# Fixed byte offsets between the weight buffers and the moving buffers of a hybrid encoder block

## The chip, the cores and the metric

The kernel runs on one core of one Trainium2 chip. The metric is device time in microseconds (us) of one execution, the median of several; "the profiled execution" is one further execution, recorded by the hardware profiler.

## What is computed

One layer on 256 tokens of width 2048, in float32: a SwiGLU feed-forward, a token mixer (a gated depthwise convolution beside a gated DeltaNet with 8 heads), a second SwiGLU, and a final norm. Every sub-layer is conditioned by shifts, scales and gates made from a vector c.

```
mods = (silu(c) @ w_ada + b_ada).reshape(9, 2048)
h = rmsnorm(x, n1) * (1 + mods[1]) + mods[0];  x += 0.5 * mods[2] * ((silu(h @ wg1) * (h @ wu1)) @ wd1)
h = rmsnorm(x, n2) * (1 + mods[4]) + mods[3];  p = h @ w_in
x += mods[5] * (concat(conv_group(p), deltanet_group(p)) @ w_out)
h = rmsnorm(x, n3) * (1 + mods[7]) + mods[6];  x += 0.5 * mods[8] * ((silu(h @ wg2) * (h @ wu2)) @ wd2)
out = rmsnorm(x, nf)
```

The weight matrices are 2048x5632 (twice) and 5632x2048 in each feed-forward, 2048x6160 into the mixer and 2048x2048 out of it.

## The kernel before

Features lie on the 128 partitions, tokens in the free dimension (T = 256), so x is 16 tiles of 128x256. Weights stream from HBM as 1 MB tiles `raw` (`weights`, L123). `split` (L110) takes half of one, 128 x 8 x 128 floats, and makes two float32r tiles of it: `hi` on ScalarE (L113) and `lo`, the remainder, on VectorE (L115). The activations are split in the same way: an `h` tile holds the normed and modulated input of 128 features, its hi half first and its lo half behind it (`h_make` L232, `h_pre` L249, both from `h_tile` L244), and an `act` tile holds the gated product of the feed-forward (`ffn_evac` L292, `put_split` L287).

A product of two split operands is three matmuls, `mm3` (L139): L142 is (weight hi, moving hi), L143 is (weight hi, moving lo), L144 is (weight lo, moving hi). The 128x128 weights are the stationary operand, loaded by one LDWEIGHTS before each matmul; the 256 tokens are the moving operand. So from one product to the next the weights that are loaded are hi, hi, lo, hi, hi, lo, and the moving halves are hi, lo, hi.

`mm3` is called from four places that differ in how often the moving tile changes:
- `col_tile` (L344): for one output tile, 16 k tiles after each other; every three matmuls go to the next h tile. The rest of both feed-forwards' gate and up products, and the mixer's input products, are of this kind.
- the second product of a feed-forward (`ffn`, L318): the same with 22 act tiles.
- `first` (L382), the first 20 column tiles of feed-forward 1: 8 weight tiles, so 24 matmuls, for one h tile, then the next.
- `group` (L265): 6 weight tiles, so 18 matmuls, for one h tile, at the start of the mixer and of feed-forward 2; the moving rows are 258 wide there.
Together 3744 products take an h tile as the moving operand and 1408 an act tile: 15456 matmuls. (1920 of them are those of `first`.) Another 112 products of plain float32 (L888) make part of the mixer's output.

The order of the work is the tile framework's schedule of this program; TensorE runs its matmuls in that order, one queue for each engine. Loads are on SyncE's queue (`load`, L118). The weights of the conditioning (`ada`, L205) are read beside the rest at a rate set in units of weight halves (`tick`, L86).

**Where the buffers lie.** Pools are laid one behind the other in the order in which they are opened (L62 to L69), every tile of a pool at the next multiple of 32 bytes, per partition: `raw` 4 x 8192 bytes, `hi` 3 x 4096, `lo` 3 x 4096, `h` 16 x 2112, `tmp` (10 tiles of 1024 bytes, two for `rb` and one for `dg` among them, and 2 of 512), `small` 832 bytes, and then, while a feed-forward runs, `act` 22 x 2048. All sizes up to h are multiples of 256 bytes but that of an h tile, 2112 = 8 x 256 + 64. Every slice of 128 weights is 512 bytes on, and a moving lo half 1024 bytes on, so slices don't change a place modulo 256. Call **offset** the place of the weights less that of the moving rows, modulo 256. Before the change it is the same for hi and lo: 0, 192, 128 and 64 for h buffers 0, 1, 2, 3 and so on in fours, and 192 for every act buffer, as 832 is 64 more than a multiple of 256. In `group` the moving lo half lies 8 bytes further.

In the gate and up products of the two feed-forwards the h tiles take these offsets in the order 192, 0, 64, 128 from one k tile to the next. (In `first` four k in a row use the same four kinds of buffer, but tiles of any two offsets can come next to each other.) The trace gives no addresses, but its matmuls stand in the program's order, so each one's offset is known from the program: the four h tiles that `first` goes through from 135.48 us of the span have the offsets 128, 192, 0 and 64, the tile from 56.69 us has 64 after one of 192, and the k tiles from 1621.86 us have 128, 192, 0, 64 and 128. What is counted as a matmul's offset is that of the weights loaded beside it, which are the next matmul's.

Other tiles that the change touches: `dg` and `rb` of `token_rsqrt` (L180: the reciprocal root of a mean square, spread over the partitions by a matmul with ones), called five times; `cacc`, the sum of the convolution's channels (L536 to L539), and `om`, a constant matrix (L544), both in `conv_norm` (L542), which takes mean and variance of the convolution while the plain float32 matmuls of L888 run; `acc`, the running sum of squares (`squares`, L309).

Of the kernel before, what the change touches and what calls it, by code (L numbers as in the profile page):

```python
# [8 lines left out]
F32 = mybir.dt.float32  # L9
F32R = mybir.dt.float32r  # L10
I32 = mybir.dt.int32
AF = mybir.ActivationFunctionType
# [3 lines left out]
P = 128  # L16
T = 256
D = 2048
# [3 lines left out]
FH = FT // 2  # L22
# [8 lines left out]
VISITS = [(g, a[g], b[g]) for a, b in zip(((0,) * NG,) + ROUNDS, ROUNDS) for g in (range(NG)[::-1] if b is ROUNDS[-1] else range(NG)) if a[g] < b[g]]  # L31
ORDER = [g * 4 + j for g, _, end in VISITS if end == 8 for j in range(4)] + list(range(4 * NG, FH))
EPS = 1e-6

PARAMS = [
    ("b_ada", 144), ("n1", 16), ("n2", 16), ("n3", 16), ("nf", 16), ("w_dw", 8 * TAPS), ("b_dw", 8),
# [15 lines left out]
class Body:  # L52
    def __init__(self, ctx, tc, x, c, prm, e0, w_ada, wa1, gu1, wd1, wk, w_in, w_ba, w_out, gw2, gu2, wd2, out):
        nc = tc.nc
        self.nc, self.tc = nc, tc
        self.x_d, self.c_d, self.prm_d, self.e0_d, self.ada_d = x, c, prm, e0, w_ada
        self.wa1_d, self.wk_d, self.w_in_d, self.w_ba_d, self.w_out_d, self.gw2_d, self.out_d = wa1, wk, w_in, w_ba, w_out, gw2, out
        self.gu_d, self.wd_d = (gu1, gu2), (wd1, wd2)
        self.bg, self.credit, self.ready = [], 0.0, 0
        self.n = 0  # L60
        self.ordered = True
        pool = lambda name, bufs, **kw: ctx.enter_context(tc.tile_pool(name=name, bufs=bufs, **kw))  # L62
        self.pers = pool("pers", 1)
        self.rawp = pool("rawp", 4)
        self.hip = pool("hip", 3)
        self.lop = pool("lop", 3)
        self.hp = pool("hp", 16)
        self.tmp = pool("tmp", 2)
        self.small = pool("small", 2)  # L69
        self.mm = pool("mm", 4, space=bass.MemoryType.PSUM)  # L70
        self.aux = pool("aux", 2, space=bass.MemoryType.PSUM)
        self.auxd = pool("auxd", 2, space=bass.MemoryType.PSUM)
        self.dram = pool("scr", 1, space=bass.MemoryType.DRAM)

    def nm(self, s):
        self.n += 1
        return f"{s}{self.n}"
# [102 lines left out]
    def token_rsqrt(self, parts, col, beside=False, raw=False):  # L180

        nc = self.nc
        ps = self.bank(self.aux)
        for i, part in enumerate(parts):
            for s in range(2):
                nc.tensor.matmul(ps[:, s:s + 1], lhsT=part[:, s * P:(s + 1) * P], rhs=col, start=i == 0 and s == 0,
                                 stop=i == len(parts) - 1 and s == 1)
        v = self.tile(self.small, [P, 2], "nv")
        nc.vector.tensor_scalar(out=v, in0=ps[:, 0:2], scalar1=EPS, scalar2=None, op0=ALU.add)
        r = self.rsqrt(v, 2, "n", beside=beside)  # L190
        dg = self.tile(self.tmp, [P, 2, P], "dg", bufs=1)
        for s in range(2):
            if beside:
                nc.scalar.activation(out=dg[:, s, :], in_=self.ident, func=AF.Copy, scale=r[:, s:s + 1])
            else:
                nc.vector.tensor_scalar(out=dg[:, s, :], in0=self.ident, scalar1=r[:, s:s + 1], scalar2=None, op0=ALU.mult)
        pb = self.bank(self.aux)
        nc.tensor.matmul(pb[:, 0:T], lhsT=self.ones, rhs=dg, start=True, stop=True)
        if raw:
            return pb[:, 0:T]  # L200
        rb = self.tile(self.tmp, [P, T], "rb")
        self.normed = nc.scalar.activation(out=rb, in_=pb[:, 0:T], func=AF.Copy)
        return rb

# [39 lines left out]
    def h_tile(self, extra=0):  # L244

        n = T + extra
        return self.tile(self.hp, [P, 2 * T + 16], "h", F32R)[:, 0:2 * n].rearrange("p (g t) -> p g t", g=2)

    def h_pre(self, k, scale, shift):  # L249

# [273 lines left out]
    def conv_taps(self, j, xs):  # L524
        nc = self.nc
        acc = self.tile(self.cva, [P, T], "cva")
        w = lambda i: self.prm[:, PSPAN["w_dw"]][:, j * TAPS + i:j * TAPS + i + 1]
        nc.scalar.activation(out=acc, in_=xs, func=AF.Identity, scale=w(TAPS - 1), bias=self.prm[:, PSPAN["b_dw"]][:, j:j + 1])  # L528
        for i in range(1, TAPS):
            after = None if i > 1 or j < 2 else self.solved if j < 4 else self.taps[j - 2]  # L530
            with self.tc.issue_after(after.ins) if after is not None else nullcontext():
                self.taps[j] = nc.vector.scalar_tensor_tensor(out=acc[:, i:T], in0=xs[:, 0:T - i], scalar=w(TAPS - 1 - i),  # L532
                                                               in1=acc[:, i:T], op0=ALU.mult, op1=ALU.add)
            yield 0.33
        if j == 0:
            self.cacc = self.tile(self.mx, [P, T], "cacc")  # L536
            nc.gpsimd.tensor_copy(out=self.cacc, in_=acc)
        else:
            nc.gpsimd.tensor_tensor(out=self.cacc, in0=self.cacc, in1=acc, op=ALU.add)  # L539
        self.cv[j] = acc  # L540

    def conv_norm(self):  # L542
        nc = self.nc
        om = self.tile(self.mx, [P, P], "om")  # L544
        nc.gpsimd.memset(om, 2.0 / D)  # L545
        pm = self.bank(self.aux)
        nc.tensor.matmul(pm[:, 0:T], lhsT=om, rhs=self.cacc, start=True, stop=True)
        mu = self.tile(self.tmp, [P, T], "rb")
        nc.scalar.activation(out=mu, in_=pm[:, 0:T], func=AF.Copy)
        acc = self.tile(self.tmp, [P, T], "acc", bufs=1)  # L550
        for j in range(8):
            nc.vector.tensor_tensor(out=self.cv[j], in0=self.cv[j], in1=mu, op=ALU.subtract)
            self.sq_acc(acc, self.cv[j], j == 0)
            yield 0.7
        rb = self.token_rsqrt([acc], self.col2)
        yield 3.0
        for j in range(8):
            t = self.cv[j]
            nc.vector.tensor_tensor(out=t, in0=t, in1=rb, op=ALU.mult)
            nc.scalar.activation(out=t, in_=t, func=AF.Silu, scale=self.prm[:, PSPAN["ln_w"]][:, j:j + 1],  # L560
                                 bias=self.prm[:, PSPAN["ln_b"]][:, j:j + 1])
            y = self.h_tile()
            self.put_split(y, t)
            self.y[j] = y
            yield 0.8
# [15 lines left out]
    def l2(self, heads, tag, pool):  # L581
# [7 lines left out]
        v = self.tile(self.mx, [P, 16], tag + "v")  # L589
        nc.vector.tensor_scalar(out=v, in0=ps[:, 0:16], scalar1=EPS, scalar2=None, op0=ALU.add)  # L590
        return self.rsqrt(v, 16, tag, self.mx, True)
# [143 lines left out]
    def dn_out(self):  # L735
# [4 lines left out]
        for b in range(2):  # L740
# [50 lines left out]
            for s in range(2):  # L791
                u0 = (b + 2 * s) * 4
                nc.gpsimd.tensor_tensor(out=sc[:, s * 4:s * 4 + 4], in0=on[:, s * 4:s * 4 + 4], in1=self.rq2[:, u0:u0 + 4], op=ALU.mult)
            nc.gpsimd.tensor_scalar(out=sc, in0=sc, scalar1=1.0 / P, scalar2=EPS, op0=ALU.mult, op1=ALU.add)
            r = self.rsqrt(sc, 8, "o", beside=True)
# [110 lines left out]
    def all(self):  # L906
        nc, tc = self.nc, self.tc
        self.rate = 0.0
        n = self.norms = {}
        with tc.tile_pool(name="actp", bufs=FH) as self.actp, tc.tile_pool(name="spp", bufs=2) as self.spp, \  # L910
                tc.tile_pool(name="adap", bufs=2) as self.adap:
            self.start()
            self.bg = [self.ada_task(2), self.ada_task(4, n["n2"]), self.ada_task(3), self.ada_task(5), self.ada_task(6)]
            done = self.first()
            self.rate = 0.44
            self.ffn(0, 2, done, lambda m: self.h_pre(m, 4, 3))
            self.drain()
        self.ordered = False
        self.mix(lambda m: self.h_pre(m, 7, 6))
        with tc.tile_pool(name="actp2", bufs=FH) as self.actp, tc.tile_pool(name="spq", bufs=6) as self.spq:  # L920
            made = self.group(self.gw2_d, self.parts, 7, 6, lambda: self.tile(self.spq, [P, T], "hq"))
            done = [self.ffn_evac(t, u, b, v) for (t, b), (u, v) in zip(made, made)]
            self.rate = 0.25
            self.bg, self.credit = [self.ada_task(8)], -5
            self.ffn(1, 8, done, self.weigh)
            rb = self.token_rsqrt(self.parts, self.col, raw=True)
            for a, b in OUTS:
                xs = self.x[:, a:b, :]
                nc.vector.tensor_tensor(out=xs, in0=xs, in1=rb.unsqueeze(1).broadcast_to([P, b - a, T]), op=ALU.mult)
                nc.sync.dma_start(out=self.out_d[:, a:b, :], in_=xs)  # L930
# [67 lines left out]
```

## Time and profile before

| | us |
|---|---|
| median of 3 executions | 2008.81 (2008.69 to 2009.64) |
| the profiled execution, its own time | 2007.74 |
| its span in the trace | 2005.7 |
| TensorE busy | 1961.9, 98% |
| VectorE busy | 1494.8, 75% |
| ScalarE busy | 914.8, 46% |
| GpSimd busy | 99.3, 5% |

The profiled execution's own time is 2.0 us longer than its span (start and end of the program), and 1.1 us below the median. [...] Matmul durations in the trace (0.28 us) overlap, since matmuls are pipelined: how fast they follow each other is read from their start times, or from the count in a stretch.

### The profile page before, as it was taken

How to read it: one execution, taken by the hardware profiler on the slowest of the kernel's cores; microseconds unless marked ns; L12 is line 12 of the kernel's file. 1: busy time of each engine (PE TensorE's matmuls, PEld its weight loads, DVE VectorE, ACT ScalarE, POOL GpSimd, SP SyncE). 2: the span in 40 equal slices, each digit the busy share in tenths (PEclk: the TensorE clock that was granted, in tenths of full speed). 3: DMA queues.
4: the chain of work that ended last, by engine and by line, in shares of the span. 5: the costliest groups of instructions: out<-in, count | busy, mean ns of one | idle time of the engine just before them, and what ended most of it. 6: DMA issues, size and time to landing. Idle time of an engine off the chain costs nothing.

```text
span 2005.7 us, 38407 instructions
## 1 busy us (share of the span) xinstructions
PE 1961.9 (98%) x16206; PEld 1941.3 (97%) x16206; DVE 1494.8 (75%) x2191; ACT 914.8 (46%) x1298; POOL 99.3 (5%) x192
## 2 busy tenths in 40 slices
PE   5999999999999999999999899999999999999997
PEld 4999999999999999999999899999999999999997
DVE  6989898878777898899999977766764444444554
ACT  3444543344444444754556345544443344444442
POOL 1000000000000000070022300000000000000000
PEclk9999999999999999999999999999999999999998
DMA  8988688988989887457654265567775555555552
GB/s 321 391 342 341 247 336 336 349 343 324 352 312 355 313 339 295 179 185 268 232 189 140 95 260 184 175 243 280 268 284 186 188 189 189 180 181 187 190 189 85
DMA packets 71087, 503.63 MB, mean 251 GB/s; under 512 B 8321, under 2 KB 8961, under 8 KB 10497
## 3 DMA queue, kind: packets, MB, share of 16 engines
q1 hardware_dynamic: 69554, 499.60, 66.3%
q8 instruction: 127, 2.08, 0.4%
q0 software_dynamic: 1360, 1.58, 0.3%
q14 instruction: 46, 0.38, 0.0%
HBM read 498.52 MB, written 2.62 MB: 250 GB/s over the span
## 4 chain that ended last, share of the span: by engine, by line
PE 90%; DVE 3%; POOL 3%; ACT 1%; DMA 1%; issue 1%; DVEq 0%; SPq 0%; ACTq 0%; POOLq 0%
PE ps L142 29%; PE ps L144 29%; PE ps L143 28%; PE ps L888 3%; DVE lo L115 1%; PE ps L666 1%; POOL dt L500 1%; DMA raw<-in_w_ada 1%; ACT hi L113 1%; DVE cva L532 0%; DMA raw<-in_wa 0%; DVE kq L237 0%; DVE raw L209 0%; POOL cacc L539 0%; DMA x<-in_x 0%
## 5 line engine op out<-in xcount | busy, mean ns | idle before, releaser
L113 ACT ACTIVATE hi<-raw 128x1024 fp32r<-128x1024 f32 x643 | 680.9, 1060 | 958.6 <-PE ps L143 799.5
L115 DVE TENSOR_TENSOR lo<-raw,hi 128x1024 fp32r<-128x1024 f32 x643 | 785.3, 1222 | 431.7 <-ACT hi L113 430.6
L142 PE MATMUL ps<-h,hi 128*128 128x256 f32 (+1 forms) x3744 | 1048.3, 283 | 6.7 <-ACT hi L113 3.4
L143 PE MATMUL ps<-h,hi 128*128 128x256 f32 (+1 forms) x3744 | 1048.0, 282 | 3.1 <-DVE h L240 3.1
L144 PE MATMUL ps<-h,lo 128*128 128x256 f32 (+1 forms) x3744 | 1027.8, 282 | 0.9 <-DVE lo L115 0.8
L142 PEld LDWEIGHTS ps<-h,hi 128*128 128x128 f32 x3744 | 704.4, 189 | 8.6 <-ACT h L239 4.2
L143 PEld LDWEIGHTS ps<-h,hi 128*128 128x128 f32 x3744 | 706.7, 189 | 5.0 <-DVE h L240 3.6
L144 PEld LDWEIGHTS ps<-h,lo 128*128 128x128 f32 x3744 | 694.5, 188 | 3.1 <-DVE lo L115 1.6
L143 PE MATMUL ps<-act,hi 128*128 128x256 f32 x1408 | 392.4, 280 | 0.0
L142 PE MATMUL ps<-act,hi 128*128 128x256 f32 x1408 | 391.2, 279 | 0.0
L144 PE MATMUL ps<-act,lo 128*128 128x256 f32 x1408 | 390.1, 279 | 0.0
L209 DVE CUSTOM_DVE_ANT_0 raw<-raw,cb 128x2048 f32<-128x2048 f32 x144 | 328.7, 2284 | 5.2 <-DMA raw<-in_w_ada 5.2
L142 PEld LDWEIGHTS ps<-act,hi 128*128 128x128 f32 x1408 | 264.4, 188 | 0.0
L143 PEld LDWEIGHTS ps<-act,hi 128*128 128x128 f32 x1408 | 264.0, 188 | 0.0
L144 PEld LDWEIGHTS ps<-act,lo 128*128 128x128 f32 x1408 | 262.4, 187 | 0.1
L532 DVE SCALAR_TENSOR_TENSOR cva<-xz,prm,cva 128x251 f32<-128x251 f32 (+15 forms) x240 | 104.9, 477 | 1.2 <-ACT cva L528 0.7
L306 DVE SCALAR_TENSOR_TENSOR x<-ps,mods,x 128x256 f32<-128x256 f32 x96 | 46.0, 480 | 30.7 <-PE ps L144 29.0
L888 PE MATMUL ps<-xz,raw 128*128 128x256 f32 x224 | 51.4, 390 | 0.0
L888 PEld LDWEIGHTS ps<-xz,raw 128*128 128x128 f32 x224 | 43.6, 196 | 6.4 <-DVE xz L816 0.3
L545 POOL MEMSET om<- 128x128 f32 x1 | 0.2, 205 | 766.6 <-DVE mods L216 766.6
L290 DVE TENSOR_TENSOR act<-fg,act 128x256 fp32r<-128x256 f32 x88 | 36.7, 417 | 0.0
L289 ACT ACTIVATE act<-fg 128x256 fp32r<-128x256 f32 x88 | 35.4, 402 | 1.0 <-DVE fg L297 1.0
(234 smaller groups left out, 802.5 us busy)
## 6 DMA issues: line engine op xcount, KB each, us to landing
raw<-in_w_ada SPq DMA_DIRECT2D x144, 1024.0 KB, 5.8
raw<-in_gu SPq DMA_DIRECT2D x130, 1024.0 KB, 4.9
raw<-in_wd SPq DMA_DIRECT2D x88, 1024.0 KB, 4.9
raw<-in_w_in SPq DMA_DIRECT2D x42, 1024.0 KB, 5.0
raw<-in_wa SPq DMA_DIRECT2D x40, 1024.0 KB, 8.2
raw<-in_w_out SPq DMA_DIRECT2D x16, 1024.0 KB, 4.8
raw<-in_wk SPq DMA_DIRECT2D x6, 1024.0 KB, 6.9
raw<-in_gw SPq DMA_DIRECT2D x6, 1024.0 KB, 4.9
```

What stands on the lines that cost most here:

```text
L113: nc.scalar.activation(out=hi, in_=raw, func=AF.Copy)
L115: nc.vector.tensor_tensor(out=lo, in0=raw, in1=hi.bitcast(F32), op=ALU.subtract)
L142: nc.tensor.matmul(out, lhsT=whi, rhs=rhi, start=start, stop=False)
L143: nc.tensor.matmul(out, lhsT=whi, rhs=rlo, start=False, stop=False)
L144: nc.tensor.matmul(out, lhsT=wlo, rhs=rhi, start=False, stop=stop)
L209: nc.vector.tensor_tensor_reduce(out=w, in0=w, in1=self.cb, scale=1.0, scalar=0.0, op0=ALU.mult, op1=ALU.add, accum_out=self.macc[:, n:n + 1])
L289: nc.scalar.activation(out=dst[:, 0, 0:T], in_=src, func=AF.Copy)
L290: nc.vector.tensor_tensor(out=dst[:, 1, 0:T], in0=src, in1=dst[:, 0, 0:T].bitcast(F32), op=ALU.subtract)
L306: self.nc.vector.scalar_tensor_tensor(out=xm, in0=ps, scalar=self.mods[:, gate * 16 + m:gate * 16 + m + 1], in1=xm, op0=ALU.mult, op1=ALU.add)
L500: nc.gpsimd.tensor_scalar(out=gs[:, i, :], in0=self.low, scalar1=g2[:, b * 4 + i:b * 4 + i + 1], scalar2=None, op0=ALU.mult)
L532: self.taps[j] = nc.vector.scalar_tensor_tensor(out=acc[:, i:T], in0=xs[:, 0:T - i], scalar=w(TAPS - 1 - i), in1=acc[:, i:T], op0=ALU.mult ...
L888: nc.tensor.matmul(ps, lhsT=w[:, k, :], rhs=self.zs[k], start=k == 0, stop=k == 7)
```

## The change

The hi pool is followed by 128 bytes of padding, the lo pool by 192 bytes, and an h tile is 2304 = 9 x 256 bytes instead of 2112. In each feed-forward 192 bytes stand ahead of the act tiles. So hi lies at 192 and lo at 64 bytes modulo 256 from every h and act buffer, in place of four offsets in turn for h (the same for hi and lo) and 192 for both with act. The pads are tiles of their own, each written once by a GpSimd memset. To make room, `dg` takes a buffer of tag `ht`, `rb` has one buffer instead of two, `cacc` takes the one buffer of `acc`, and `om` goes: the matmul of `conv_norm` takes `ones`, and the factor 2/D is put into the ScalarE copy behind it.

```diff
@@ -31,6 +31,8 @@
 VISITS = [(g, a[g], b[g]) for a, b in zip(((0,) * NG,) + ROUNDS, ROUNDS) for g in (range(NG)[::-1] if b is ROUNDS[-1] else range(NG)) if a[g] < b[g]]
 ORDER = [g * 4 + j for g, _, end in VISITS if end == 8 for j in range(4)] + list(range(4 * NG, FH))
 EPS = 1e-6
+HI, LO, MOVING = 0, 128, 64
+ACT = 192
 
 PARAMS = [
     ("b_ada", 144), ("n1", 16), ("n2", 16), ("n3", 16), ("nf", 16), ("w_dw", 8 * TAPS), ("b_dw", 8),
@@ -63,7 +65,9 @@
         self.pers = pool("pers", 1)
         self.rawp = pool("rawp", 4)
         self.hip = pool("hip", 3)
+        self.pad(pool("pad1", 1), LO - HI)
         self.lop = pool("lop", 3)
+        self.pad(pool("pad2", 1), MOVING - LO)
         self.hp = pool("hp", 16)
         self.tmp = pool("tmp", 2)
         self.small = pool("small", 2)
@@ -71,6 +75,11 @@
         self.aux = pool("aux", 2, space=bass.MemoryType.PSUM)
         self.auxd = pool("auxd", 2, space=bass.MemoryType.PSUM)
         self.dram = pool("scr", 1, space=bass.MemoryType.DRAM)
+
+    def pad(self, pool, size):
+
+        if size % 256:
+            self.nc.gpsimd.memset(pool.tile([P, size % 256 // 4], F32, name=self.nm("pad")), 0.0)
 
     def nm(self, s):
         self.n += 1
@@ -188,7 +197,7 @@
         v = self.tile(self.small, [P, 2], "nv")
         nc.vector.tensor_scalar(out=v, in0=ps[:, 0:2], scalar1=EPS, scalar2=None, op0=ALU.add)
         r = self.rsqrt(v, 2, "n", beside=beside)
-        dg = self.tile(self.tmp, [P, 2, P], "dg", bufs=1)
+        dg = self.tile(self.tmp, [P, T], "ht").rearrange("p (s t) -> p s t", s=2)
         for s in range(2):
             if beside:
                 nc.scalar.activation(out=dg[:, s, :], in_=self.ident, func=AF.Copy, scale=r[:, s:s + 1])
@@ -198,7 +207,7 @@
         nc.tensor.matmul(pb[:, 0:T], lhsT=self.ones, rhs=dg, start=True, stop=True)
         if raw:
             return pb[:, 0:T]
-        rb = self.tile(self.tmp, [P, T], "rb")
+        rb = self.tile(self.tmp, [P, T], "rb", bufs=1)
         self.normed = nc.scalar.activation(out=rb, in_=pb[:, 0:T], func=AF.Copy)
         return rb
 
@@ -244,7 +253,7 @@
     def h_tile(self, extra=0):
 
         n = T + extra
-        return self.tile(self.hp, [P, 2 * T + 16], "h", F32R)[:, 0:2 * n].rearrange("p (g t) -> p g t", g=2)
+        return self.tile(self.hp, [P, 2 * T + 64], "h", F32R)[:, 0:2 * n].rearrange("p (g t) -> p g t", g=2)
 
     def h_pre(self, k, scale, shift):
 
@@ -533,7 +542,7 @@
                                                                in1=acc[:, i:T], op0=ALU.mult, op1=ALU.add)
             yield 0.33
         if j == 0:
-            self.cacc = self.tile(self.mx, [P, T], "cacc")
+            self.cacc = self.tile(self.tmp, [P, T], "acc", bufs=1)
             nc.gpsimd.tensor_copy(out=self.cacc, in_=acc)
         else:
             nc.gpsimd.tensor_tensor(out=self.cacc, in0=self.cacc, in1=acc, op=ALU.add)
@@ -541,12 +550,10 @@
 
     def conv_norm(self):
         nc = self.nc
-        om = self.tile(self.mx, [P, P], "om")
-        nc.gpsimd.memset(om, 2.0 / D)
         pm = self.bank(self.aux)
-        nc.tensor.matmul(pm[:, 0:T], lhsT=om, rhs=self.cacc, start=True, stop=True)
-        mu = self.tile(self.tmp, [P, T], "rb")
-        nc.scalar.activation(out=mu, in_=pm[:, 0:T], func=AF.Copy)
+        nc.tensor.matmul(pm[:, 0:T], lhsT=self.ones, rhs=self.cacc, start=True, stop=True)
+        mu = self.tile(self.tmp, [P, T], "rb", bufs=1)
+        nc.scalar.activation(out=mu, in_=pm[:, 0:T], func=AF.Copy, scale=2.0 / D)
         acc = self.tile(self.tmp, [P, T], "acc", bufs=1)
         for j in range(8):
             nc.vector.tensor_tensor(out=self.cv[j], in0=self.cv[j], in1=mu, op=ALU.subtract)
@@ -907,8 +914,9 @@
         nc, tc = self.nc, self.tc
         self.rate = 0.0
         n = self.norms = {}
-        with tc.tile_pool(name="actp", bufs=FH) as self.actp, tc.tile_pool(name="spp", bufs=2) as self.spp, \
+        with tc.tile_pool(name="pad3", bufs=1) as pad, tc.tile_pool(name="actp", bufs=FH) as self.actp, tc.tile_pool(name="spp", bufs=2) as self.spp, \
                 tc.tile_pool(name="adap", bufs=2) as self.adap:
+            self.pad(pad, ACT)
             self.start()
             self.bg = [self.ada_task(2), self.ada_task(4, n["n2"]), self.ada_task(3), self.ada_task(5), self.ada_task(6)]
             done = self.first()
@@ -917,7 +925,8 @@
             self.drain()
         self.ordered = False
         self.mix(lambda m: self.h_pre(m, 7, 6))
-        with tc.tile_pool(name="actp2", bufs=FH) as self.actp, tc.tile_pool(name="spq", bufs=6) as self.spq:
+        with tc.tile_pool(name="pad4", bufs=1) as pad, tc.tile_pool(name="actp2", bufs=FH) as self.actp, tc.tile_pool(name="spq", bufs=6) as self.spq:
+            self.pad(pad, ACT)
             made = self.group(self.gw2_d, self.parts, 7, 6, lambda: self.tile(self.spq, [P, T], "hq"))
             done = [self.ffn_evac(t, u, b, v) for (t, b), (u, v) in zip(made, made)]
             self.rate = 0.25
```

## Rows read from the trace of the kernel before

**Rows 1.** The page's busy times, and TensorE's granted clock in 40 slices.
```profile
span 2005.7 us, 38407 instructions
PE 1961.9 (98%) x16206; PEld 1941.3 (97%) x16206; DVE 1494.8 (75%) x2191; ACT 914.8 (46%) x1298; POOL 99.3 (5%) x192
...
PEclk9999999999999999999999999999999999999998
```

**Rows 2.** The page's chain that ended last, by engine and by line.
```profile
PE 90%; DVE 3%; POOL 3%; ACT 1%; DMA 1%; issue 1%; DVEq 0%; SPq 0%; ACTq 0%; POOLq 0%
PE ps L142 29%; PE ps L144 29%; PE ps L143 28%; PE ps L888 3%; DVE lo L115 1%; PE ps L666 1%; POOL dt L500 1%; DMA raw<-in_w_ada 1%; ACT hi L113 1%; DVE cva L532 0%; DMA raw<-in_wa 0%; DVE kq L237 0%; DVE raw L209 0%; POOL cacc L539 0%; DMA x<-in_x 0%
```

**Rows 3.** The view of waits: who waited for whom, us in total, times, longest.
```profile
ACT hi L113 <- PE ps L143: 799.5, 490, 6.0
...
DVE lo L115 <- ACT hi L113: 430.6, 393, 2.0
...
ACT rb L549 <- PE ps L547: 15.7, 1, 15.7
```

**Rows 4.** Windows of stages: busy us and count of each engine, clock, DMA share, GB/s.
```profile
core 0: us, PE busy (x) PEld busy (x) DVE busy (x) ACT busy (x) POOL busy (x), PEclk, DMA share, GB/s
...
412.80:663.70 250.90, 250.90 (x2113) 250.90 (x2112) 201.26 (x236) 105.59 (x131) 0.00 (x0) 1.00 0.87 332
663.90:788.10 124.20, 124.20 (x1056) 124.20 (x1056) 110.53 (x158) 59.54 (x91) 0.00 (x0) 1.00 0.88 340
1491.10:1615.20 124.10, 124.10 (x1056) 124.10 (x1055) 63.06 (x65) 47.26 (x46) 0.00 (x0) 1.00 0.55 198
1615.50:1866.40 250.90, 250.90 (x2112) 250.90 (x2112) 122.28 (x131) 105.46 (x130) 0.00 (x0) 1.00 0.52 185
1866.60:1990.70 124.10, 124.10 (x1056) 124.10 (x1056) 63.19 (x73) 57.85 (x74) 0.00 (x0) 1.00 0.43 153
```

**Rows 5.** Timeline of TensorE in `first`: start us, us, engine, line, operands.
```profile
135.48 0.28 PE L142 MATMUL ps<-h,hi 128*128 128x256 f32 x1
...
138.33 0.28 PE L142 MATMUL ps<-h,hi 128*128 128x256 f32 x1
...
141.16 0.29 PE L142 MATMUL ps<-h,hi 128*128 128x256 f32 x1
...
144.04 0.29 PE L142 MATMUL ps<-h,hi 128*128 128x256 f32 x1
...
144.40 0.28 PE L142 MATMUL ps<-h,hi 128*128 128x256 f32 x1
...
146.78 0.28 PE L142 MATMUL ps<-h,hi 128*128 128x256 f32 x1
```

**Rows 6.** The same view, earlier in `first`.
```profile
56.69 0.28 PE L142 MATMUL ps<-h,hi 128*128 128x256 f32 x1
...
59.16 0.28 PE L142 MATMUL ps<-h,hi 128*128 128x256 f32 x1
```

**Rows 7.** Timeline of TensorE in the gate and up products of feed-forward 2.
```profile
1621.86 0.29 PE L142 MATMUL ps<-h,hi 128*128 128x256 f32 x1
...
1622.22 0.28 PE L142 MATMUL ps<-h,hi 128*128 128x256 f32 x1
...
1622.57 0.28 PE L142 MATMUL ps<-h,hi 128*128 128x256 f32 x1
...
1622.92 0.29 PE L142 MATMUL ps<-h,hi 128*128 128x256 f32 x1
...
1623.28 0.29 PE L142 MATMUL ps<-h,hi 128*128 128x256 f32 x1
```

**Rows 8.** The page's groups: busy us, mean ns | idle before, releaser.
```profile
L545 POOL MEMSET om<- 128x128 f32 x1 | 0.2, 205 | 766.6 <-DVE mods L216 766.6
```

**Rows 9.** The chain in order of time: start us, us, what.
```profile
1028.23 1.78 PE ps L666 x16
...
1144.16 16.84 PE ps L888 x78
```

## The prediction

> **What bounds the kernel now.** First the page's busy times [rows 1]: TensorE works for 98% of the span, at the full granted clock. The chain of work that ended last says the same [rows 2]: 86% of it are the three matmuls of `mm3` (L142 to L144). In the view of waits the longest entry is ScalarE's hi waiting for a matmul, 799.5 us in all, and VectorE's lo waits for that hi [rows 3]: the split weights are made as soon as TensorE gives a buffer back, so nobody feeds it too slowly. What counts is how fast matmuls follow each other.
>
> That is read from stages without a stall [rows 4]. The gate and up stages of both feed-forwards hold 22 x 2 x 16 x 3 = 2112 matmuls on h tiles and take 250.9 us: 118.8 ns for one. The stages on act tiles hold 22 x 16 x 3 = 1056 and take 124.1 to 124.2 us: 117.5 to 117.6, which I take as 117.7, since the window's edges are rounded inwards by up to two matmuls. [...] VectorE is 80 to 89% busy and DMA 87% in the first two of these stages, 49 to 51% and 43 to 55% in the later ones, and the pace doesn't differ. So neither sets it, and something is left that tells h from act: by the buffers' places, act has offset 192 always, h has 192, 0, 64 and 128 in turn.
>
> `first` shows the offsets apart, as 24 matmuls in a row keep one h tile. The five starts of [rows 5] that stand 24 matmuls apart belong to offsets 128, 192, 0 and 64: 2.85, 2.83, 2.88 and 2.74 us, which is 118.8, 117.9, 120.0 and 114.2 ns. At 64 the first three are slow; from the fourth, at 144.40, to the end 21 matmuls take 2.38 us, 113.3 each. This is the fastest pace of this shape that I find in the trace. It isn't always reached: in [rows 6] 21 matmuls at offset 64 follow an h tile at 192, and take 2.47 us, 117.6 each, without ever speeding up. So the pace depends on the offset and on what went before. With the h tile changing every three matmuls the four offsets make one round of 12 matmuls from 1621.86 to 1623.28 [rows 7]: 1.42 us, 118.5 ns by the two rounded ends (118.8 by the whole stage), where the mean of the four in `first` would be 117.7. So changing costs about 1 ns for each matmul over keeping.
>
> **The change part by part.** The padding makes all h and act buffers alike. Weights load beside the matmul before theirs: each product then has, one after the other, a load of hi beside a moving hi (offset 192), a load of lo beside a moving lo (64), and the next product's hi beside a moving hi (192). Between 113.3 and 120.0 ns, the ends that [rows 5] show, I take the mean that the two offsets have where each is by itself, (117.7 + 117.7 + 113.3) / 3 = 116.2 ns, since both are known rows and two of three loads keep an offset that all act stages use now.
>
> The sum, by matmuls: of the 15456, 4224 are on act (1408 x 3), 1920 in `first`, and 9312 on h elsewhere. The 9312 go from 118.8 to 116.2: 24.2 us less. `first` goes from the mean of its four offsets, 117.7, to 116.2: 2.9 us. Act goes from 117.7 to 116.2: 6.3 us. Together 33.4 us. I count every matmul, though a few per cent stand at stalls of the mixer, where a faster pace buys waiting; VectorE, at 89% in the dearest stage, would be at 90%, DMA at 0.89, and both have room.
>
> The rest of the edit I cost at nothing, within 1 us either way. Pads: four GpSimd memsets, smaller than the 0.2 us of the one for `om` that goes [rows 8]; two at the start, two ahead of the feed-forwards, where GpSimd does nothing [rows 4] and nobody waits for it. One `rb` buffer adds a wait on ScalarE, with the splits of the next weights queued behind it: but the `rb` that follows the mean (L549) is made from sums that need all eight reads of that mean, so it is late anyway, and the other calls of `token_rsqrt` lie hundreds of us apart. If that cover were gone, a hi would be late by one VectorE pass, under 1 us. `dg` in an `ht` buffer waits for squares that its own input needs. `cacc` in `acc`: the first square of `conv_norm` must wait for the matmul of L547, but it reads a channel less the mean, and the mean comes from that matmul; TensorE meanwhile runs L888, 78 matmuls without a gap in 16.84 us [rows 9], and ScalarE's wait there, 15.7 us [rows 3], stays. The weights and moving rows of L888 shift to another offset too. They run at 215.9 ns each; I take no change, as their moving rows are read at half the pace, and bound it by the spread of [rows 5], 6% from 113.3 to 120.0, of the 48 us of all 224: 2.9 us either way. No step moves to another queue, and no DMA is added.
>
> So 2007.7 (the profiled execution) less 33.4 is 1974.3, and the median stands 1.1 above that execution: **1975.4 us**.
>
> [...] The rows say that only places in memory differ between 113.3 and 120.0. [...]
>
> **The rivals.**
> 1. The fast pace of 64 is never reached, as in [rows 6]: two of three loads are at 192, and coming from 192 the 64 ran at 117.6. Then all goes at 117.7: 9312 x 1.1 = 10.2 us less, 1998.6. For it: [rows 6] come nearest to what the change makes. Against it: there the moving tile, not the weights, changed place.
> 2. The pair settles into the fast pace, as 21 matmuls in a row do in [rows 5]: 113.3 for all is 9312 x 5.5 + 6144 x 4.4 = 78.2 us less, 1930.6. A floor is the pace of weight loads beside short matmuls, 16 in 1.78 us, 111.3 each [rows 9]; 9312 x 7.5 + 6144 x 6.4 = 109 us less would be 1899.6, and I see no row that comes near it with 256 moving rows. VectorE at 89% would become 93%.
> 3. Slower: changing the offset is what costs. Now act never changes it, and h every third matmul; after the change every product does so twice, between 192 and 64. The price is that of the change of tile in [rows 7] taken twice, or about the worst pace, 120.0 [rows 5]: 9312 x 1.2 + 6144 x 2.3 = 25.3 us more, 2034.1. It decides where the mean passes today's, (9312 x 118.8 + 6144 x 117.7) / 15456 = 118.4 ns. Against it: the round with four changes of tile costs only 1 ns over the mean.
> [...]
>
> **How the numbers follow.** Forecast 0.42, rival 1 0.24, rival 2 0.14, rival 3 0.14, rival 4 0.06. Forecast and rivals 1 and 2 hold 0.80; the range takes them in with the bounds of the small terms (3.9 us together) and some way towards the floor: 1925 to 2003. About 0.2% is what a measurement of this kernel can tell from no change, 4 us: faster is the forecast with rivals 1 and 2, 0.80; the same is rival 4, 0.06; slower is rival 3, 0.14.
>
> **What would show it.** In the stages of [rows 4] the same counts should take about 245.4 us (2112) and 122.7 us (1056): equal paces for h and act, which is the part that I am surest of. 248.6 and 124.3 would be rival 1, 239.3 and 119.6 rival 2, over 251 rival 3. The 24 matmuls of one h tile in `first` should all take the same time, about 2.79 us. I am wrong if h and act still differ, or if stalls grow: VectorE's lo ending last ahead of TensorE, or `rb` and `acc` in the waits of the mixer.

## Result and the profile after

The changed kernel takes 1955.89 us (median of 4 executions, 1953.11 to 1957.27) against 2009.22 us for the kernel before on the same chip (4 executions, 2008.69 to 2010.71): a ratio of 0.9732, 95% interval 0.9715 to 0.9749, or 53 us less. The forecast was 1975.4, 33 us less; the range held it. The profiled execution took 1953.11 us, its span is 54.4 us shorter than that of [rows 1].

The page after: busy times, and the chain that ended last, by engine. (In the lines further down, L151 to L153 are the old L142 to L144.)
```profile
span 1951.3 us, 38411 instructions
PE 1906.5 (98%) x16206; PEld 1885.9 (97%) x16206; DVE 1493.9 (77%) x2191; ACT 916.2 (47%) x1298; POOL 97.0 (5%) x195
...
PE 90%; DVE 4%; POOL 2%; ACT 2%; DMA 1%; issue 1%; DVEq 0%; SPq 0%; ACTq 0%; POOLq 0%
```
TensorE is still the bound, with the same 16206 matmuls and 98% busy, against [rows 1, 2]. So the time came out of the pace of matmuls, not out of waits. The waits that answer to [rows 3]:
```profile
ACT hi L122 <- PE ps L152: 743.9, 485, 7.5
DVE lo L124 <- ACT hi L122: 382.1, 370, 2.1
...
ACT rb L556 <- PE ps L554: 15.5, 1, 15.5
```
ScalarE waits 56 us less for TensorE, as buffers come back sooner; no new wait took its place, and the one for the mean (L556) is what it was (15.7).

The stages that answer to [rows 4], with `first` ahead of them and the mixer between (columns as in [rows 4]):
```profile
26.60:280.10 253.50, 245.11 (x2089) 243.42 (x2090) 229.60 (x313) 120.98 (x159) 0.00 (x0) 0.99 0.86 336
403.60:642.80 239.20, 239.20 (x2114) 239.20 (x2112) 201.16 (x236) 105.75 (x131) 0.00 (x0) 1.00 0.92 349
642.90:762.40 119.50, 119.50 (x1057) 119.50 (x1056) 110.29 (x158) 59.81 (x91) 0.00 (x0) 1.00 0.90 356
763.00:1457.20 694.20, 686.36 (x5614) 674.61 (x5615) 577.57 (x1047) 356.93 (x597) 89.19 (x170) 0.99 0.59 213
1457.40:1577.20 119.80, 119.80 (x1056) 119.80 (x1056) 63.04 (x65) 47.32 (x46) 0.00 (x0) 1.00 0.57 204
1577.40:1816.60 239.20, 239.20 (x2113) 239.20 (x2112) 122.33 (x131) 105.55 (x130) 0.00 (x0) 1.00 0.55 194
1816.80:1936.30 119.50, 119.50 (x1056) 119.50 (x1056) 63.11 (x73) 57.94 (x74) 0.00 (x0) 1.00 0.44 159
```
The kernel before took in `first` and in the stretch around the mixer (from the end of the act stage of [rows 4] at 788 us to the start of the next at 1491):
```profile
26.60:285.50 258.90, 251.14 (x2089) 249.50 (x2090) 231.26 (x315) 120.74 (x160) 0.00 (x0) 1.00 0.84 330
...
788.60:1490.90 702.30, 694.69 (x5615) 682.78 (x5615) 577.38 (x1046) 356.60 (x597) 91.61 (x170) 1.00 0.58 211
```
The two stages of 2112 give 11.7 us each, the three of 1056 4.7, 4.3 and 4.6, `first` 5.4, the 5600 matmuls around the mixer only 8.1, and what lies between `first` and 403.6 us 3.8: 54 in all. 239.2 us for 2112 matmuls is 113.3 ns, and 119.5 for 1056 is 113.2: h and act go alike, and both at the fastest pace that the kernel before showed for a few us.

Yet it isn't one pace for the whole kernel. TensorE alone, in three stretches without a stall (us, count, clock, DMA share, GB/s; a count includes two or three matmuls cut by the edges):
```profile
320.00:750.00 430.00, 430.00 (x3796) 1.00 0.91 350
...
1260.00:1440.00 180.00, 180.00 (x1517) 1.00 0.71 261
1480.00:1900.00 420.00, 420.00 (x3708) 1.00 0.55 194
```
The first and the last go at 113.3. The one in the middle belongs to the same products (`col_tile`, 192, 64, 192) with the same buffers, and goes at 118.8, no faster than before. By the start times, 1872 matmuls in a row, from 1240.5 to 1463.1 us, stand 118.9 apart on average. The other half of the same gate and up products, from 1577 us on, goes at 113.3. Why the same layout has two paces is the question of the experiments.

### The profile page after: what moved, and what is told of

It is laid out like the page before. It is cut to its first block, busy times and chain, and to the rows that moved or that the text cites. A ratio compares the mean times of both kernels' runs of the same rounds, so it can differ in the third digit from the quotient of the medians.

```text
span 1951.3 us, 38411 instructions
## 1 busy us (share of the span) xinstructions
PE 1906.5 (98%) x16206; PEld 1885.9 (97%) x16206; DVE 1493.9 (77%) x2191; ACT 916.2 (47%) x1298; POOL 97.0 (5%) x195
## 4 chain that ended last, share of the span: by engine, by line
PE 90%; DVE 4%; POOL 2%; ACT 2%; DMA 1%; issue 1%; DVEq 0%; SPq 0%; ACTq 0%; POOLq 0%
PE ps L152 28%; PE ps L153 28%; PE ps L151 28%; PE ps L895 3%; DVE lo L124 1%; DMA raw<-in_w_ada 1%; DVE raw L218 1%; PE ps L673 1%; POOL dt L509 1%; ACT hi L122 1%; DVE kq L246 0%; DVE h L249 0%; DMA x<-in_x 0%; PE ps L195 0%; DVE x L938 0%
## 5 line engine op out<-in xcount | busy, mean ns | idle before, releaser
L152 PE MATMUL ps<-h,hi 128*128 128x256 f32 (+1 forms) x3744 | 1038.0, 280 | 3.2 <-DVE h L249 3.2
L151 PE MATMUL ps<-h,hi 128*128 128x256 f32 (+1 forms) x3744 | 1030.8, 279 | 7.8 <-ACT hi L122 4.5
L153 PE MATMUL ps<-h,lo 128*128 128x256 f32 (+1 forms) x3744 | 1015.6, 278 | 0.4 <-DVE lo L124 0.2
L151 PEld LDWEIGHTS ps<-h,hi 128*128 128x128 f32 x3744 | 702.8, 188 | 9.8 <-ACT hi L122 4.9
L152 PEld LDWEIGHTS ps<-h,hi 128*128 128x128 f32 x3744 | 703.6, 188 | 5.0 <-DVE h L249 3.6
L153 PEld LDWEIGHTS ps<-h,lo 128*128 128x128 f32 x3744 | 693.5, 188 | 2.5 <-DVE lo L124 1.2
L152 PE MATMUL ps<-act,hi 128*128 128x256 f32 x1408 | 387.2, 276 | 0.0
L151 PE MATMUL ps<-act,hi 128*128 128x256 f32 x1408 | 387.0, 276 | 0.0
L153 PE MATMUL ps<-act,lo 128*128 128x256 f32 x1408 | 386.1, 276 | 0.0
L151 PEld LDWEIGHTS ps<-act,hi 128*128 128x128 f32 x1408 | 264.2, 188 | 0.0
L152 PEld LDWEIGHTS ps<-act,hi 128*128 128x128 f32 x1408 | 264.0, 188 | 0.0
L153 PEld LDWEIGHTS ps<-act,lo 128*128 128x128 f32 x1408 | 263.2, 188 | 0.3 <-DVE lo L124 0.2
L895 PE MATMUL ps<-xz,raw 128*128 128x256 f32 x224 | 50.9, 387 | 0.0
L895 PEld LDWEIGHTS ps<-xz,raw 128*128 128x128 f32 x224 | 43.2, 195 | 6.3 <-DVE xz L823 0.3
```

The source lines that it names most:

```text
L151: nc.tensor.matmul(out, lhsT=whi, rhs=rhi, start=start, stop=False)
L152: nc.tensor.matmul(out, lhsT=whi, rhs=rlo, start=False, stop=False)
L153: nc.tensor.matmul(out, lhsT=wlo, rhs=rhi, start=False, stop=stop)
L895: nc.tensor.matmul(ps, lhsT=w[:, k, :], rhs=self.zs[k], start=k == 0, stop=k == 7)
```

## The experiments

The theories: (1) the pair of offsets sets the pace; (2) h buffers that are all alike are enough, whatever the offset; (3) the small edits did it. Every kernel below differs from the changed one only by its diff, of which the telling lines are shown. In all traces but those of the four kernels that change the order or `group`, TensorE's matmuls stand in the same order as in the kernel before, so no difference below comes from the schedule. HI, LO and MOVING are places modulo 256; with MOVING a multiple of 256, HI and LO are the offsets themselves, and a pad ahead of the hi pool (`pad0`, in all kernels of that kind) brings hi there. The moving rows then lie at a multiple of 256, as they do in the changed kernel.

**The small edits alone.**
```diff
-HI, LO, MOVING = 0, 128, 64
-ACT = 192
+HI, LO, MOVING = 0, 0, 0
+ACT = 0
-        return self.tile(self.hp, [P, 2 * T + 64], "h", F32R)[:, 0:2 * n].rearrange("p (g t) -> p g t", g=2)
+        return self.tile(self.hp, [P, 2 * T + 16], "h", F32R)[:, 0:2 * n].rearrange("p (g t) -> p g t", g=2)
```


> Only the edits of rb, dg, cacc and om; no padding, h buffers of 2112 bytes, so all offsets as before. Theory 1: no change, 2009 us within 2 us, the gate and up stages at 118.9 ns. Theory 3 (these edits did it): 1956 us.

2008.83 us (10 executions, 2005.99 to 2010.62), ratio 0.9995 [0.9985, 1.0004]. Theory 3 is out: `rb`, `dg`, `cacc` and `om` are worth nothing that can be measured.

**Both at 192, and both at 64.**
```diff
-HI, LO, MOVING = 0, 128, 64
+HI, LO, MOVING = 192, 192, 256
+        self.pad(pool("pad0", 1), HI - 192)
```


> All of the change, but lo at 192 like hi (no padding between the pools, 64 bytes behind lo), so that every matmul has the offset that all act matmuls had before. Theory 1 (the pace is set by the pair of offsets, and 192 with 64 is what lets it lock at 113.3 ns): everything runs at the old act pace of 117.8 ns, the gate and up stages take 248.7 us and the act stages 124.3; the time is 2009 less about 10 to 15, some 1994 to 1999 us. Theory 2 (it is enough that all h buffers lie alike, the padding between hi and lo does nothing): as the changed kernel, 1956 us. Theory 3 (the edits of rb, dg, cacc and om did it): 1956 us as well.

```diff
+HI, LO, MOVING = 64, 64, 256
```


> All of the change, but hi and lo both at 64. Theory 1 in its simple form (each matmul has the pace of its own offset): 113.3 ns throughout, at least as fast as the changed kernel, about 1930 to 1956 us. Theory 1 with two paces for one offset (before, 64 was seen at 113.3 and at 117.6): stages stick at either, by what went before; 1940 to 2000 us, with whole stages at 117.6 to 119 ns. That only 192 with 64 locks: no stage at 113.3, about 1998 us.

Both at 192: 1998.2 us, but its 10 executions go from 1980.7 to 2002.98, ratio 0.9932 [0.9907, 0.9957]. Both at 64: 1955.34, from 1941.31 to 1967.94 in 4, ratio 0.9728 [0.9672, 0.9783]. Such a spread was not seen in the kernel before (2005.79 to 2012.1 in 19 executions beside them). TensorE in the profiled execution of 192 (1980.7 us):
```profile
320.00:750.00 430.00, 430.00 (x3797) 1.00 0.90 349
...
1480.00:1900.00 420.00, 420.00 (x3568) 1.00 0.52 188
```
and in that of 64 (1967.94 us):
```profile
320.00:750.00 430.00, 430.00 (x3653) 1.00 0.88 336
...
1480.00:1900.00 420.00, 420.00 (x3708) 1.00 0.55 197
```
3797 in 430 us is 113.3 ns, 3653 is 117.8. So 192 by itself can go at 113.3, as long as 4032 matmuls, and 64 by itself can stay at 117.8 for 4104. Theory 1, by which 192 costs 117.7, does not hold in this form: each of the two offsets has both paces. With 192 the fast stretch is worth 4032 x 4.45 ns = 17.9 us, and 1980.7 + 17.9 = 1998.6 is close to the median: most executions may miss it, but only the fastest one has a trace. Theory 2 is out as well: here all h buffers are alike, and the time is 1998.2, not 1956.

**Both at 64 once more.** The same kernel, for a second profile.

> The kernel with hi and lo both at 64 once more, unchanged (its four runs went from 1941.3 to 1967.9 us; in its first profile 4104 matmuls in a row at 117.8 and 6000 at 113.3). Theory A: the stretches between two interruptions are at one of the same two paces, 113.3 or 117.8, but other stretches may be the slow ones; a run in which all of them are fast gives about 1942 us, one with the 4104 slow 1942 + 4104 x 4.45 ns = 1960 us or more. Theory 1 (the offset alone sets the pace): the same stretches at the same paces as in the first profile.

1947.71 us, in one execution on another chip; the four above, all on one chip, spread further than that. The same stretches:
```profile
320.00:750.00 430.00, 430.00 (x3797) 1.00 0.90 350
900.00:980.00 80.00, 80.00 (x681) 1.00 0.65 241
...
1480.00:1900.00 420.00, 420.00 (x3709) 1.00 0.53 194
```
What went at 117.8 in the first profile goes at 113.3 in this one (the mixer's stretch from 900 us is slow here). So one and the same program takes either pace in one and the same stage, and keeps it until something interrupts it. That is theory A: a layout offers a fast and a slow pace, and a stage keeps the one it fell into.

What interrupts it can be found by the start times. The last change of pace ahead of the long stretch stands at the same matmul in both profiles, one that comes late because its weights do. In the first profile it starts 0.57 us after the matmul ahead of it:
```profile
292.47 0.28 PE L153 MATMUL ps<-act,hi 128*128 128x256 f32 x1
293.04 0.38 PE L154 MATMUL ps<-act,lo 128*128 128x256 f32 x1 [0.30 <-DVE lo L125]
```
in the second 0.22 us after it:
```profile
296.00 0.28 PE L153 MATMUL ps<-act,hi 128*128 128x256 f32 x1
296.22 0.38 PE L154 MATMUL ps<-act,lo 128*128 128x256 f32 x1
```
Ahead of the wait the first profile goes at 113.3 and the second at 117.8, behind it the other way round. In the four profiles with one offset for all (these two, both at 192, and both at 192 with the turn below), every change between the two paces stands at such a wait (an interval over 140 ns) or at `group`, counted between stretches of 12 matmuls and more.

**The order of one product in sixteen.** In the changed kernel the slow stretch ends in the midst of the act products:
```profile
1464.48 0.28 PE L151 MATMUL ps<-act,hi 128*128 128x256 f32 x1
1464.60 0.28 PE L152 MATMUL ps<-act,hi 128*128 128x256 f32 x1
1464.72 0.28 PE L153 MATMUL ps<-act,lo 128*128 128x256 f32 x1
1464.84 0.40 PE L151 MATMUL ps<-act,hi 128*128 128x256 f32 x2
1465.07 0.28 PE L152 MATMUL ps<-act,hi 128*128 128x256 f32 x1
```
Nothing stalls there; the schedule runs two first matmuls (L151, x2) of different products behind each other, which breaks the series 192, 64, 192. It is the first such break since 1241 us. Around it (the same columns for TensorE):
```profile
1440.00:1464.00 24.00, 24.00 (x204) 1.00 0.75 270
1466.00:1490.00 24.00, 24.00 (x214) 1.00 0.63 235
```
If such a break heals (ends the slow pace), it can be put in by hand: the ninth product of a column tile takes its three matmuls in another order. (`first`, which the expectation names, and the mixer's output product, which the list of four places leaves out, call `mm3` themselves and keep their order.)
```diff
+        if turned:
+            nc.tensor.matmul(out, lhsT=whi, rhs=rhi, start=start, stop=False)
+            nc.tensor.matmul(out, lhsT=wlo, rhs=rhi, start=False, stop=False)
+            nc.tensor.matmul(out, lhsT=whi, rhs=rlo, start=False, stop=stop)
+            return
...
+                self.mm3(ps, hi[:, k, :], lo[:, k, :], self.rhs(self.h[kk]), kk == 0, kk == 15, kk == 8)
```


> The changed kernel with the ninth product of every column tile in another order (hi with hi, lo with hi, hi with lo instead of hi-hi, hi-lo, lo-hi), so the same matmuls, but the series of offsets is broken once per 48 matmuls of the gate/up and first stages. Theory A: two steady paces exist for one and the same layout (113.3 and about 118.9 ns), a stage keeps the one it entered with, and a change in the series of offsets lets it drop into 113.3. Then the stretch 1220 to 1466 us of the changed kernel (2064 matmuls at 118.9) runs at 113.3 from its first broken tile on: 2064 x 5.6 ns = 11.5 us less, 1943 to 1946 us. Theory B: the slow stretch comes from what else goes on in it (DMA, vector work), not from the series: 1955 to 1957 us. A break that throws a fast stage into the slow pace would give over 1957 us.

1944.18 us (1941.76 to 1946.28), ratio 0.9672 [0.9657, 0.9687]: 11.7 us under the changed kernel, where 11.5 was expected. The stretch that was slow:
```profile
1260.00:1440.00 180.00, 180.00 (x1590) 1.00 0.73 275
```
1590 instead of 1517: 113.3 ns. Its DMA and vector work go on as before, a little faster, so theory B is out. The trace shows the moment: up to the first turned product of the stage (L152 to L154) matmuls start 119 ns apart, from 1246.2 us on 113.3, without a wait:
```profile
1245.50 0.28 PE L158 MATMUL ps<-h,lo 128*128 128x256 f32 x1
1245.62 0.28 PE L152 MATMUL ps<-h,hi 128*128 128x256 f32 x1
1245.74 0.28 PE L153 MATMUL ps<-h,lo 128*128 128x256 f32 x1
1245.86 0.28 PE L154 MATMUL ps<-h,hi 128*128 128x256 f32 x1
```
Not all of it went one way: in this profile the mixer's output product, which isn't turned, goes at 118.9 from 1161 to 1203 us, where the changed kernel's went at 113.3 (2 us more).

The same turn with both at 192, where a change of order changes no offset (A3 is the rival that any change of order heals):

> The kernel with hi and lo both at 192 (1998.2 us; in its profile 4032 matmuls at 113.3 and 6024 at 117.8, each without a break) with the ninth product of every column tile in the other order, as in the run with the changed kernel. Theory A as it stands (what heals is a change in the series of offsets): with one offset for all the order changes nothing in the series, so the same two paces are kept where they are: 1980 to 2003 us. Theory A3 (any change of the order of weights lets the pace fall): the long slow stretches go to 113.3, 1945 to 1960 us.

1998.87 us (10 executions, 1978.62 to 2002.97), against 1998.2 without it. The last stretch stays slow:
```profile
1480.00:1900.00 420.00, 420.00 (x3568) 1.00 0.51 188
```
So it isn't the order of the weights that heals but a change in the series of offsets. Both at 64 says the same without any turn: some 40 places of its slow stretch from 297 to 778 us, in the first profile, have the schedule's own changes of order, and it stays at 117.8. With one offset for everything no change of order ended a slow stage in these traces, which fits their spread from run to run.

**What throws the stage into the slow pace.** In `group`, just before it, the moving lo half lies 8 bytes off. Here it is put at byte 1280, and the two shift columns of that half are left out:
```diff
+        t = self.tile(self.hp, [P, 2 * T + 64], "h", F32R)
+        if extra:
+            return t[:, 0:n], t[:, T + 64:2 * T + 64]
...
```


> The changed kernel with the lo half of the 258-wide h tiles of the mixer put at byte 1280 (a multiple of 256) instead of 8 bytes behind such a multiple; the products of the lo halves of the two shift columns are left out (two columns of the lo pass). Theory A1: the 8 bytes by which the lo half lies off its place in that group (pace 121 ns there) throw the following gate/up stage into the slow pace. Then it runs at 113.3: 11.5 us less, and the group itself some 168 matmuls x up to 7 ns = 1 us, so 1942 to 1945 us. Theory A2: any interruption can do it, and the entry is decided by the phase at that moment: anything between 1943 and 1956 us.

1954.76 us (1953.24 to 1960.85), ratio 0.9730 [0.9711, 0.9750]: no gain, and 1516 matmuls from 1260 to 1440 us. A1 falls: the 8 bytes are not what does it. What else in `group` does stays open. Elsewhere the traces of this layout (the change, the turn and this run) show a stage go from 113.3 to 118.9 only behind a wait (counted as above); none of some 300 breaks at 113.3 does it, and of 14 breaks at 118.9 all but 3 end that pace.

**Hi and lo swapped.**
```diff
+HI, LO, MOVING = 64, 192, 256
```


> All of the change, but hi at 64 and lo at 192. Two of three loads have the fast offset now instead of one. By each matmul's own offset it would be faster than the changed kernel, (2 x 113.3 + 117.8) / 3 = 114.8 ns or better, 1930 to 1956 us. If it is the turn of 192 and 64 in the order hi, hi, lo that locks, it is slower than the changed kernel, 1975 to 2010 us.

1945.18 us (1944.06 to 1947.86), ratio 0.9681 [0.9666, 0.9695]: faster than the changed kernel, as the intervals do not meet. The series is now 64, 192, 64, and every long stage falls into the fast pace by itself, so the order hi, hi, lo of 192 and 64 isn't needed for it:
```profile
320.00:750.00 430.00, 430.00 (x3797) 1.00 0.90 350
...
1260.00:1440.00 180.00, 180.00 (x1591) 1.00 0.74 275
1480.00:1900.00 420.00, 420.00 (x3709) 1.00 0.54 194
```
With the turned product as well:

> The swapped layout (hi at 64, lo at 192; 1945.2 us, in its profile nearly all at 113.3) with the ninth product of each column tile in the other order. Theory A: nothing is left to heal in the long stages, so 1942 to 1947 us, and no run above it. If the breaks cost a pace of their own (221 tiles or so, each a few ns): 1 us more at most.

1943.19 us (1939.86 to 1947.12), ratio 0.9668 [0.9652, 0.9683]. Nothing was left to heal (one execution is 0.1 over the expected range), and this can't be told from either edit alone (1944.18, 1945.18). All three beat both kernels.

**Other offsets.**
```diff
+HI, LO, MOVING = 0, 128, 256
```


> The changed kernel with hi at offset 0 and lo at offset 128 from the moving rows, the two places that went with 120.0 and 118 to 119 ns in the kernel before. Theory 1 (the byte offset sets what paces are to be had): no stretch at 113.3, mean of (0, 128, 0) about (120.0 + 118.5 + 120.0) / 3 = 119.5 ns, against 114.6 in the changed kernel: 15232 x 4.9 ns = 75 us more, 2020 to 2035 us. Theory A alone (offsets only need to follow a regular series, any offsets): 113.3 in most of it, 1943 to 1960 us.

```diff
+HI, LO, MOVING = 160, 32, 256
```


> The changed kernel with hi at offset 160 and lo at 32, halfway between the places of the changed kernel (192, 64) and the slow ones (128, 0). If only being off the multiples of 128 bytes matters: 113.3 in most of it, 1940 to 1960 us. If the price goes evenly with the distance: half way between 1950 and 2019.7, about 1985 us. If the offset must be 64 from a multiple of 128: 119.1 ns throughout, 2015 to 2022 us.

```diff
+HI, LO, MOVING = 192, 128, 256
```


> The changed kernel with hi at 192 and lo at 128: two of three matmuls stand at an offset that can go at 113.3 and one at one that went at 118 to 119. If each matmul has its own price: (113.3 + 118.7 + 113.3) / 3 = 115.1 ns, about 1963 us. If one bad offset in the series keeps all of it out of 113.3: 117.8 to 119.1 ns for all, 2000 to 2020 us.

0 with 128: 2019.69 us (2019.21 to 2020.42), 1.0048 [1.0033, 1.0063], 0.5% slower than before. 160 with 32: 2020.5 (2020.32 to 2024.87), 1.0057 [1.0042, 1.0072]. 192 with 128: 1982.56 (1979.16 to 1984.05), 0.9859 [0.9843, 0.9876]. TensorE with 0 and 128:
```profile
320.00:750.00 430.00, 430.00 (x3611) 1.00 0.87 335
...
1480.00:1900.00 420.00, 420.00 (x3528) 1.00 0.53 192
```
with 160 and 32:
```profile
1260.00:1440.00 180.00, 180.00 (x1487) 1.00 0.63 234
1480.00:1900.00 420.00, 420.00 (x3560) 1.00 0.54 196
```
with 192 and 128:
```profile
320.00:750.00 430.00, 430.00 (x3668) 1.00 0.89 339
...
1480.00:1900.00 420.00, 420.00 (x3637) 1.00 0.53 193
```
With 0 and 128 every long stage goes at 119.1, breaks or not, so theory A alone (any regular series will do) falls: the places decide which paces are to be had. And it is the place of one against the other: the kernel before had its weights at one place and went by that of the moving rows, these kernels have the moving rows at one place and go by that of the weights. Half way, at 160 and 32, there are two again, 121.1 and 117.8, none at 113.3; the price is not even in the distance. And with one of three at 128 the last stretch goes at 115.6, close to the 115.1 of a price for each matmul, and long parts of the earlier ones at 117.8; the time came between the two that had been expected.

In these two a break doesn't only heal. With 192 and 128 the same stage goes at 115.6 up to a pair of breaks at 445 to 448 us, and at 117.8 behind it:
```profile
408.00:444.00 36.00, 36.00 (x314) 1.00 0.96 348
449.00:501.00 52.00, 52.00 (x444) 1.00 0.87 330
```
Between the two breaks of the later pairs, for 21 matmuls, it is back at 115.5. With 160 and 32 the pair at 447 to 450 us is followed by 121.1 in place of 117.8, and the break in the act stage at 1514 us by 117.8 in place of 121.1. So a break can end either pace; that it throws no stage out of the fast one holds for 192 and 64 in turn alone.

By the start times of the matmuls, in long stretches without a stall:

| hi, lo | fast | slow | time, us |
|---|---|---|---|
| 64, 192 | 113.3 ns | none in a long stage | 1945.2 |
| 192, 64 (the change) | 113.3 | 118.9 | 1955.9 |
| 64, 64 | 113.3 | 117.8 | 1955.3 |
| 192, 128 | 115.6 | 117.8 | 1982.6 |
| 192, 192 | 113.3 | 117.8 | 1998.2 |
| 0, 128 | none | 119.1 | 2019.7 |
| 160, 32 | 117.8 | 121.1 | 2020.5 |

## Why the prediction was right, and where it was not

**The bound** was right: TensorE's pace is the time, and neither DMA (0.92 where it was 0.87) nor VectorE (84% of the first long stage, 92% of the act stage after it) got in the way when it went faster.

**That offsets set it** was right. That the time stays the same (rival 4, 0.06) is out twice: by the time, and by seven layouts that differ in pads alone and go from 1945 to 2020 us. The pace goes from 113.3 to 121.1 ns with nothing but places changed, for matmuls of one shape (128x256) in stages with a granted clock of 1.00. What in TensorE waits, no run shows. Weights do load beside the matmul before theirs, as the prediction counts the offsets; in the kernel before:
```profile
1499.90 0.28 PE L142 MATMUL ps<-act,hi 128*128 128x256 f32 x1
1499.90 0.19 PEld L143 LDWEIGHTS ps<-act,hi 128*128 128x128 f32 x1
...
1500.02 0.28 PE L143 MATMUL ps<-act,hi 128*128 128x256 f32 x1
1500.02 0.19 PEld L144 LDWEIGHTS ps<-act,lo 128*128 128x128 f32 x1
```

**That all would go at one pace** was half right. The "equal paces for h and act" came out in the stages of [rows 4], 113.3 and 113.2, but two halves of the same gate and up products stand at 118.9 and 113.3.

**The step that failed** is the price of the pair: "the mean that the two offsets have where each is by itself, (117.7 + 117.7 + 113.3) / 3 = 116.2". 117.7 was not the price of 192 but the slower of its two paces: the act stages before never left it, having one offset and no break in its series. The run with both at 192 shows that offset at 113.3. So the term has no such mean: stages take 113.3 or 118.9. The stages of [rows 4] came out as rival 2 had them (239.3 and 119.6 expected, 239.2 and 119.5 to 119.8 measured), and `first` too: 24 matmuls that the prediction puts at 2.79 us take 2.72, from one to the 24th after it:
```profile
132.82 0.28 PE L151 MATMUL ps<-h,hi 128*128 128x256 f32 x1
...
135.54 0.28 PE L151 MATMUL ps<-h,hi 128*128 128x256 f32 x1
```
Rival 2 gave 78.2 us in all, and 54 came. By the start times: intervals without a stall went from 118.49 to 114.61 ns on average, 15456 x 3.88 = 60.0 us less. At 113.33 throughout it would have been 19.8 more, of which the one stretch of 1872 holds 1872 x 5.56 = 10.4; the two `group`s and the mixer's pieces between waits hold most of the rest. And 5.5 us went back: 220 intervals over 140 ns (the plain float32 part among them), 138.4 us over the pace, for 181 with 132.9. Most of that isn't stalls but clock: 42 of the 220 are matmuls that start some 213 ns apart while the granted clock is 0.50, from 51.5, 72.0 and 860.5 us, and hold 4.1 us; the kernel before kept 1.00 in these places. So 60.0 - 5.5 = 54.5. The forecast is 20 us short of that: it puts the stages at 113.3 too high, and makes up part of it by putting those at 118.9 too low. The range held the result since it took rival 2 in.

One reading has a slip: the round of [rows 7], 1.42 us for 12 matmuls, is 118.3 ns, not 118.5. The price of about 1 ns for changing the tile rests on the 118.8 of the whole stage, and stands.

**Rows 6 were the clue** that was read as rival 1 (stuck at 117.6 after 192). They show that 64 has two paces, which the prediction said of it ("the offset and what went before") and did not say of 192.

**Rival 3**, that changing the offset is dear, did not come: with 192 and 64 in turn nearly everything goes at 113.3, and a break in the series heals, which with one offset for all no change of order did.

**The small edits** cost nothing, as costed. The products of L888 (now L895) kept their pace: [rows 9] have 78 in 16.84 us, 215.9 ns each, where `mm3`'s matmuls of the same 128x256 took 118.8 [rows 4], and the chain after has
```profile
1112.86 16.84 PE ps L895 x78
```

## What to carry to other kernels

Where matmuls with loaded weights follow each other without a stall, compare the pace of stages with the same shape and clock; if they differ, work out the place of the weights against the moving rows, and try it with pads: here 64 with 192 modulo 256 was good (1945.2 and 1955.9 us, against 2009 before), 0 with 128 and 32 with 160 no better than before (2019.7 and 2020.5). A pace read in one stage is not yet the price of its layout, as it may be the slower of two; look for the fastest stretch of that layout anywhere, and for where a stage changes its pace. A kernel whose executions spread by 1% at full clock may be choosing between them, as both at 192 did (1980.7 to 2002.98 us). With 192 and 64 in turn, one product in sixteen in another order was enough to leave the slow pace (1590 matmuls in 180 us, 1517 without it); on the old layout this was not tried.

## What had not been expected

- The same program takes 113.3 or 117.8 ns in the same stage from one execution to the next (both at 64: 3653 and 3797 matmuls in 430 us), and keeps it for up to 6000 matmuls.
- A break in the series of offsets, at no stall, ends the slow pace of 192 and 64 (204 matmuls in 24 us ahead of it, 214 behind it). Why, and what TensorE waits for, no run shows; nor was it tried how few bytes beside 64 or 192 are still good, or how long a wait must be to change the pace.
- The first 70 us of matmuls ran at a mean granted clock of 0.95 in the changed kernel, with 473 matmuls where the kernel before had 490 at 1.00. Two short stretches, from 51.5 and from 72.0 us, have the lower clock, 0.50; they come 1.6 and 1.7 us after a wait of TensorE (3.2 and 1.8 us from start to start). The kernel before waited 2.2 and 1.8 us there and kept 1.00. The small edits alone, with the old layout, show the same 0.95 and 471, so it isn't the layout's. Changed kernel, then small edits:
```profile
26.58:97.00 70.42, 62.03 (x473) 60.34 (x474) 62.97 (x84) 30.45 (x39) 0.00 (x0) 0.95 0.90 351
26.58:97.00 70.42, 61.47 (x471) 60.04 (x472) 63.13 (x84) 30.30 (x40) 0.00 (x0) 0.95 0.89 350
```
- No stretch of `mm3`'s 256-column matmuls is faster than 113.3 ns in these traces, and none comes to the 111.3 that rival 2 takes for a floor. What holds them there, no run shows.
